# Summed weight pairs in a SwiGLU encoder block: sums on GpSimd, three of eight pairs, a new SBUF layout

## The chip, the cores and the metric

One core of a Trainium2 chip. The metric is the device time of one execution, in microseconds. Most executions of this kernel agree within a few tenths of a per cent.

## What is computed

One encoder layer on 256 tokens of width 2048, all in fp32:

```python
x = x + W_out [ MLA(h) || DiffAttn(h) ]      # h = rms_norm(x), one input projection
x = x + CrossAttn(rms_norm(x), rms_norm(mem))
hf = rms_norm(x, g_ffn)
x = x + (silu(hf @ w_gate) * (hf @ w_up)) @ w_down    # 2048 -> 5632 -> 2048
return rms_norm(x, g_final)
```

The change works in the last line but one, the feed-forward part, and in where tiles lie.

## The kernel before

**Split operands.** Each fp32 matrix is held as a high part (`h`, rounded to fp32r) and a low part (`l`, what is left). `mm` (L89) makes one product out of three matmuls: high x high (L91), high x low (L92), low x high (L93). `split_into` (L97) makes the parts: ScalarE casts the high one (L99), VectorE subtracts it from the source (L100).

**Weights.** Every weight is loaded once from HBM in pieces of 1 MB, by the SP queue, into one of three raw tiles `wraw` (128 x 2048). Two calls of `split_into` turn a raw tile into two pairs of tiles `wh` and `wl` (128 x 1024, four of each, used in turn). TensorE streams these as the moving operand; the activations, transposed and split, are the stationary one.

**The feed-forward part.** The hidden width 5632 is one narrow chunk of 512 columns and five wide chunks of 1024. A wide chunk (`wide_chunk`) is a gate pass and an up pass over eight K pairs (a pair is 256 rows of K), each pass a `wide_project`: four accumulators in PSUM, one raw tile per pair. Then silu(gate) x up is transposed into four new K pairs for the down projection. Down passes (`wide_add`) follow in three groups, after chunks 0, 1-2 and 3-4; the last 1024 output columns of the last group go through the simpler `project`.

**Plain and summed pairs.** A plain pair (kind P) is a 2 x 2 grid of blocks times a 2 x 2 grid: 8 products. A summed pair (kind W) is made in Winograd's way with 7 products from sums of blocks: `summed_pair` makes the sums of the activations once, and `wide_project` makes four sums of the weight blocks for each raw tile, on VectorE: one instruction of 1024 columns (L707) and two of 512 (L711, L712) into `tsum`. The sums have to be split too: 3.5 tiles of 1024 columns a summed pair, 2 a plain one. Of the four sums' split tiles one pair lies in a buffer of its own (`wsum`). Four of the seven products go into PSUM tiles of their own (`q`), which VectorE combines in `leave` once the last summed pair is done; `join` (L744 in gate and up passes) adds an accumulator to the result.

The kinds are `GU_KINDS = "PPWPWPPP"` for gate and up (2 of 8 summed) and `DN_KINDS = "PP" + "PPPW" * 5` for down.

**Silu.** In a wide chunk ScalarE takes the sigmoid of the gate result (L824) and VectorE multiplies it in (L825).

**GpSimd** does the angle tables at the start, small powers, and near the end the multiplication with the final gain (L870); it also issues the transfer of that gain (L865).

**Order.** Engines run their own queues in order. The order within each queue is set when the program is built, by a planner with its own cost estimates that may move instructions of independent tiles past each other. Weight loads keep the program's order (`keep_in_program_order`).

**SBUF.** Pools are laid one behind the other: `const`, then the weights `wp`, then `act` and the smaller ones; `tp`, `soft` and `wsum` are opened in turn.

Of the kernel before, what the change touches and what calls it, by code (L numbers as in the profile page):

```python
# [11 lines left out]
F32 = mybir.dt.float32  # L12
# [7 lines left out]
P = 128  # L20
# [54 lines left out]
def encoder_block(ctx: ExitStack, tc: tile.TileContext, a, out):  # L75
    nc = tc.nc
    PS = bass.MemoryType.PSUM
    const = ctx.enter_context(tc.tile_pool(name="const", bufs=1))
    wp = ctx.enter_context(tc.tile_pool(name="wp", bufs=3))
    act = ctx.enter_context(tc.tile_pool(name="act", bufs=24))  # L80
    sb = ctx.enter_context(tc.tile_pool(name="sb", bufs=2))
    small = ctx.enter_context(tc.tile_pool(name="small", bufs=4))
# [3 lines left out]
    tp = tables.enter_context(tc.tile_pool(name="tp", bufs=1))  # L86

# [19 lines left out]
    def act_tile(shape=(P, 4, S), name="act"):  # L107
# [3 lines left out]
        )  # L111

    def weights(src, fine=False, pool=None, before_k=None, cut=None, raw=None):

        nk, ncols = src.shape[1:]
        begun = raw is not None
        if not begun:  # L120
            raw = wp.tile([P, 2048], F32, name="wraw", tag="wraw", bufs=3)
        raw = raw[:, :nk * ncols].rearrange("p (k c) -> p k c", k=nk)
        step = 1 if fine else nk
        for k in range(0, nk, step):
            if before_k is not None:
                before_k(k)
            if begun and k == 0:
                continue
            tc.keep_in_program_order(nc.sync.dma_start(out=raw[:, k:k + step, :], in_=src[:, k:k + step, :]))
        ks = []  # L130
        step = max(1, 1024 // ncols // 2 * 2)
        for k in range(0, nk, step):
            n = min(step, nk - k)
            if pool:
                w = pool((P, n, ncols), "w")
            else:
                w = [wp.tile([P, 1024], F32R, name=x, tag=x, bufs=4)[:, :n * ncols].rearrange("p (k c) -> p k c", k=n)
                     for x in ("wh", "wl")]
                w = Split(*w)
# [26 lines left out]
    def nat(name):  # L166
        return sb.tile([P, 512], F32, name=name, tag="nat", bufs=7)

# [17 lines left out]
    LAT = KVL + DR  # L186
    lat_raw = wp.tile([P, 2048], F32, name="wraw", tag="wraw", bufs=3)
    for c0, c1 in ((0, QL), (QL, QL + LAT)):
# [12 lines left out]
    NF = DR // 2 + DD // 2  # L201
    posi = const.tile([P, NT], I32, name="posi")
    invf = const.tile([P, NF], F32, name="invf")
    ident = const.tile([P, P], F32, name="ident")
# [60 lines left out]

    posf = const.tile([P, NT], F32, name="posf")
    nc.gpsimd.tensor_copy(out=posf, in_=posi)
# [79 lines left out]

    cosr = const.tile([P, NT, 2, DR // 2], F32, name="cosr")
    sinr = const.tile([P, NT, 2, DR // 2], F32, name="sinr")
    cosd = const.tile([P, NT, 2, DD // 2], F32, name="cosd")  # L350
    sind = const.tile([P, NT, 2, DD // 2], F32, name="sind")

# [31 lines left out]
    soft_pool = ExitStack()  # L384
    soft = soft_pool.enter_context(tc.tile_pool(name="soft", bufs=2))

# [100 lines left out]
    for hg in range(2):  # L487
        t = act_tile(name="mixT")
        mixT.append(t)
        for hp in range(2):  # L490
            ps = [scores([qT[hg][:, h, :], qrT[:, 2 * hg + hp, :]], [kT[hg][:, h, :], krT[:, h % 2, :]])
                  for h in (2 * hp, 2 * hp + 1)]
# [13 lines left out]
                                   op0=ALU.add, op1=ALU.subtract)  # L506
    gdb = const.tile([P, DV], F32, name="gdb")
    tc.keep_in_program_order(nc.sync.dma_start(out=gdb, in_=a["g_diff_sub"].partition_broadcast(P)))
# [124 lines left out]
    soft_pool.close()  # L633
    wsum = ctx.enter_context(tc.tile_pool(name="wsum", bufs=1))


    def pair_raw(src):
        raw = wp.tile([P, 2048], F32, name="wraw", tag="wraw", bufs=3)
        raw = raw.rearrange("p (b c) -> p b c", b=4)
        tc.keep_in_program_order(nc.sync.dma_start(out=raw, in_=src))  # L640
        return raw

    def w_tile(n=2, pool=None):

        pool, tags, bufs = (wp, ("wh", "wl"), 4) if pool is None else (pool, ("wh2", "wl2"), 1)
        return Split(*[pool.tile([P, 1024], F32R, name=x, tag=x, bufs=bufs)[:, :n * 512].rearrange(
            "p (b c) -> p b c", b=n) for x in tags])

    def split_blocks(src, pool=None):
        w = w_tile(src.shape[1], pool)  # L650
        split_into(w, src)
        return w

# [26 lines left out]
    def wide_project(pairs, src, order, leave, join):  # L680

        accs = [[pacc.tile([P, 512], F32, name="acc", tag="acc") for _ in range(2)] for _ in range(NT)]
        used = [[False] * 2 for _ in range(NT)]
        summed = [i for i in order if pairs[i].forms is not None]  # L690
        Q = {}
        for n, i in enumerate(order):
            stop = n == len(order) - 1
            raw = pair_raw(src[i])
            if i not in summed:
                w = [split_blocks(raw[:, 2 * k:2 * k + 2, :]) for k in range(2)]
                for tt in range(NT):
                    for oc in range(2):
                        for k in range(2):
                            mm(accs[tt][oc], pairs[i].at(k, tt), w[k][:, oc, :], not used[tt][oc], stop and k == 1)  # L700
# [6 lines left out]
            nc.vector.tensor_tensor(out=t[:, 0:2, :], in0=raw[:, 1:3, :],  # L707
                                    in1=raw[:, 0:1, :].to_broadcast([P, 2, 512]), op=ALU.add)
            t13 = split_blocks(t[:, 0:2, :])
            b21 = split_blocks(raw[:, 3:4, :])  # L710
            nc.vector.tensor_tensor(out=t[:, 2, :], in0=t[:, 0, :], in1=raw[:, 2, :], op=ALU.add)  # L711
            nc.vector.tensor_tensor(out=t[:, 3, :], in0=t[:, 2, :], in1=raw[:, 3, :], op=ALU.add)  # L712
# [3 lines left out]
            mm(Q[1], A11, b11[:, 0, :], *own)  # L716
            mm(accs[0][1], S3, b11[:, 1, :], False, stop)
            mm(Q[5], S5, t13[:, 0, :], *own)
            mm(Q[7], S7, t13[:, 1, :], *own)
            mm(accs[0][0], A12, b21[:, 0, :], False, stop)  # L720
            mm(Q[6], S6, t24[:, 0, :], *own)
            mm(accs[1][0], A22, t24[:, 1, :], False, stop)
# [51 lines left out]
    def normalized_pairs():  # L774
# [12 lines left out]
        for i, kind in enumerate(GU_KINDS):  # L787
            xr = x2raw[i // 2][:, i % 2 * 2:i % 2 * 2 + 2, :]
            if kind == "P":
                if n == 4:  # L790
                    t, n = act_tile(name="x2n"), 0
                split_into(t[:, n:n + 2, :], xr)
                pairs.append(Pair(t[:, n:n + 2, :]))
                n += 2
            else:
                pairs.append(summed_pair(xr[:, :, :P], xr[:, :, P:]))
        return pairs

    def narrow_chunk(c):
# [5 lines left out]
        for tt in range(NT):  # L805
            r = rstdf[:, tt:tt + 1]
            sg = nat("sg")
            nc.scalar.activation(sg, ga[tt], AF.Sigmoid, scale=r)
            nc.vector.scalar_tensor_tensor(out=sg, in0=ga[tt], scalar=r, in1=sg, op0=ALU.mult, op1=ALU.mult)
            h = nat("h")  # L810
# [6 lines left out]
    def wide_chunk(c, spare):  # L817

        g = wide_result(xn, a["w_gu"][c, 0], GU_SEQ)
        for tt in range(NT):  # L820
            for oc in range(2):
                sg = nat("sg")
                gs = g[tt][:, oc, :]
                nc.scalar.activation(sg, gs, AF.Sigmoid)  # L824
                nc.vector.tensor_tensor(out=gs, in0=gs, in1=sg, op=ALU.mult)  # L825
        u = wide_result(xn, a["w_gu"][c, 1], GU_SEQ)
# [179 lines left out]
```

## Time and profile before

| what | value |
|---|---|
| median of 3 runs | 1158.55 us (1158.5 to 1159.19) |
| profiled execution | 1158.9 us, of which the span is 1157.1 us |
| TensorE / VectorE / ScalarE / GpSimd busy | 1148.1 / 901.3 / 611.0 / 69.3 us |
| granted TensorE clock | 0.999 |
| HBM read | 219.11 MB, 191 GB/s with the writes over the span |

Busy time is the time in which an engine had an instruction in it. TensorE's matmuls overlap each other, so the step from one start to the next says how fast it goes, not the duration of one. The feed-forward part runs from about 460 us to the end.

### The profile page before, as it was taken

The numbers are of one execution on the slowest core, as the hardware profiler recorded it, in microseconds if no ns is written. First come the engines' busy times: TensorE is split into PE (matmuls) and PEld (weight loads), VectorE is DVE, ScalarE is ACT, GpSimd is POOL, SyncE is SP. The second block draws the span as 40 slices with busy tenths as digits, with TensorE's granted clock in tenths as the row PEclk, the third lists the DMA queues.
The fourth block names the chain that finished last, engine by engine and source line by source line (L and its number), as shares of the span: only waits on it lengthen the run. The fifth ranks groups of instructions, "written<-read, shape, count | busy, mean of one in ns | idle before, by whom it ended". The sixth has DMA issues, their size and how long they took to land.

```text
span 1157.1 us, 14401 instructions
## 1 busy us (share of the span) xinstructions
PE 1148.1 (99%) x5510; PEld 961.7 (83%) x5510; DVE 901.3 (78%) x1197; ACT 611.0 (53%) x863; POOL 69.3 (6%) x81
## 2 busy tenths in 40 slices
PE   9999999999999999999999999999999999999997
PEld 7888888888888888888888888888888888888887
DVE  7698766586867776978888787797888788798873
ACT  6755454554665565655444554564544554554552
POOL 4920000001000000000000000000000000000021
PEclk9999999999999999999999999999999999999999
DMA  9565344435755445465565555645556555555651
GB/s 356 215 218 189 113 145 168 161 146 206 272 212 182 146 149 187 174 218 182 185 214 184 206 184 192 218 181 183 202 179 223 204 181 202 192 220 202 210 204 73
DMA packets 33764, 222.13 MB, mean 192 GB/s; under 512 B 4128, under 2 KB 4896, under 8 KB 8992
## 3 DMA queue, kind: packets, MB, share of 16 engines
q1 hardware_dynamic: 32256, 216.86, 52.4%
q0 software_dynamic: 864, 3.15, 0.7%
q10 hardware_dynamic: 576, 1.21, 0.3%
q8 instruction: 43, 0.70, 0.2%
q14 instruction: 25, 0.20, 0.1%
HBM read 219.11 MB, written 2.10 MB: 191 GB/s over the span
## 4 chain that ended last, share of the span: by engine, by line
PE 98%; DMA 1%; issue 0%; DVE 0%; SPq 0%; ACT 0%; POOLq 0%; POOL 0%; DVEq 0%; ACTq 0%
PE acc L92 28%; PE acc L91 28%; PE acc L93 28%; PE q L91 2%; PE q L92 2%; PE q L93 2%; PE pt L315 2%; PE ppt L462 1%; DMA wraw<-in_w_in_lat 1%; PE psc L93 1%; PE psc L91 1%; PE psc L92 1%; PE pt L838 0%; PE acckv L93 0%; PE acckv L92 0%
## 5 line engine op out<-in xcount | busy, mean ns | idle before, releaser
L99 ACT CAST wh<-wraw 128x1024 fp32r<-128x1024 f32 (+2 forms) x399 | 399.2, 1013 | 383.1 <-PE acc L93 346.7
L100 DVE TENSOR_TENSOR wl<-wraw,wh 128x1024 fp32r<-128x1024 f32 (+2 forms) x399 | 469.0, 1184 | 166.3 <-ACT wh L99 164.4
L92 PE MATMUL acc<-wl,x2n_h 128*128 128x512 f32 x480 | 185.5, 390 | 0.0
L93 PE MATMUL acc<-wh,x2n_l 128*128 128x512 f32 x480 | 185.2, 389 | 0.0
L91 PE MATMUL acc<-wh,x2n_h 128*128 128x512 f32 x480 | 160.3, 390 | 0.0
L93 PEld LDWEIGHTS acc<-wh,x2n_l 128*128 128x128 f32 x480 | 90.1, 188 | 18.8
L91 PEld LDWEIGHTS acc<-wh,x2n_h 128*128 128x128 f32 x480 | 90.1, 188 | 18.8
L92 PEld LDWEIGHTS acc<-wl,x2n_h 128*128 128x128 f32 x480 | 90.1, 188 | 18.7
L92 PE MATMUL acc<-wl,hT_h 128*128 128x512 f32 (+1 forms) x272 | 103.7, 381 | 0.0
L93 PE MATMUL acc<-wh,hT_l 128*128 128x512 f32 (+1 forms) x272 | 103.5, 381 | 0.0
L91 PE MATMUL acc<-wh,hT_h 128*128 128x512 f32 (+1 forms) x272 | 89.4, 382 | 0.0
L92 PE MATMUL acc<-wl,x0T_h 128*128 128x512 f32 x224 | 88.2, 395 | 0.0
L93 PE MATMUL acc<-wh,x0T_l 128*128 128x512 f32 x224 | 87.8, 393 | 0.0
L91 PE MATMUL acc<-wh,x0T_h 128*128 128x512 f32 x224 | 87.4, 396 | 0.3 <-ACT x0T_h L102 0.3
L99 ACT CAST wh<-tsum 128x1024 fp32r<-128x1024 f32 x56 | 58.3, 1047 | 42.2 <-DVE tsum L712 30.8
L100 DVE TENSOR_TENSOR wl<-tsum,wh 128x1024 fp32r<-128x1024 f32 x56 | 67.9, 1218 | 9.2 <-ACT wh L99 9.1
L91 PEld LDWEIGHTS acc<-wh,hT_h 128*128 128x128 f32 x272 | 51.2, 188 | 9.9 <-issue 0.2
L93 PEld LDWEIGHTS acc<-wh,hT_l 128*128 128x128 f32 x272 | 51.2, 188 | 9.6
L92 PEld LDWEIGHTS acc<-wl,hT_h 128*128 128x128 f32 x272 | 51.2, 188 | 9.4
L91 PEld LDWEIGHTS acc<-wh,x0T_h 128*128 128x128 f32 x224 | 42.2, 189 | 9.2 <-ACT x0T_h L102 1.2
L92 PEld LDWEIGHTS acc<-wl,x0T_h 128*128 128x128 f32 x224 | 42.3, 189 | 7.9 <-DVE wl L100 0.4
L93 PEld LDWEIGHTS acc<-wh,x0T_l 128*128 128x128 f32 x224 | 42.2, 188 | 7.6
(363 smaller groups left out, 2005.9 us busy)
## 6 DMA issues: line engine op xcount, KB each, us to landing
wraw<-in_w_gu SPq DMA_DIRECT2D x80, 1024.0 KB, 4.8
wraw<-in_w_dn SPq DMA_DIRECT2D x36, 1024.0 KB, 4.8
wraw<-in_w_in SPq DMA_DIRECT2D x24, 1024.0 KB, 4.8
wraw<-in_w_out SPq DMA_DIRECT2D x16, 1024.0 KB, 4.8
wraw<-in_w_down SPq DMA_DIRECT2D x8, 1024.0 KB, 4.8
wraw<-in_w_in_lat SPq DMA_DIRECT2D x7, 832.0 KB, 7.8
wraw<-in_w_xk SPq DMA_DIRECT2D x4, 1024.0 KB, 6.1
wraw<-in_w_xq SPq DMA_DIRECT2D x4, 1024.0 KB, 4.8
```

Of the source, the lines that this page charges most:

```text
L91: nc.tensor.matmul(o, l.h, r.h, start=start, stop=False)
L92: nc.tensor.matmul(o, l.h, r.l, start=False, stop=False)
L93: nc.tensor.matmul(o, l.l, r.h, start=False, stop=stop)
L99: last_cast[0] = nc.scalar.copy(out=dst.h, in_=src).ins
L100: last_split[0] = nc.vector.tensor_tensor(out=dst.l, in0=src, in1=dst.h.bitcast(F32), op=ALU.subtract).ins
L315: nc.tensor.transpose(out=pt[:, j * P:(j + 1) * P], in_=src[:, j * P:(j + 1) * P], identity=ident)
L462: nc.tensor.transpose(out=pt[:, kt * S + tt * P:kt * S + (tt + 1) * P], in_=p[:, tt, kt * P:(kt + 1) * P], identity=ident)
```

## The change

Five things change together.

1. The four weight sums of a summed pair are made by GpSimd, as four instructions of 512 columns, one of them in place in the raw tile. The order of blocks in the raw tile (`SUMS`) and of the products changes with it.
2. `GU_KINDS` has a third summed pair, in gate and up: 3 of 8.
3. In the feed-forward part there are 4 raw tiles and 5 tiles each of `wh` and `wl`, where there were 3 and 4, and the separate buffer for the last sums is gone. A class `Ring` hands the tiles out in turn and takes in the additional ones when attention's memory is free. There are two `tsum` tiles of 1024 columns and one of 512.
4. Pools are put at two ends of SBUF: split weights first at the low end (`side="left"`), with what attention needs above them, in the pool `early`; the rest at the other end. After attention `early` is closed and `late` takes its place. Scratch tiles `nat` are 7 in `early` and 3 in `late`.
5. ScalarE's own silu takes the place of sigmoid and VectorE's multiplication.

```diff
-GU_KINDS = "PPWPWPPP"
+GU_KINDS = "PPWPWPWP"
...
-PLAIN, SUMS = ((0, 0), (0, 1), (1, 0), (1, 1)), ((0, 1), (0, 0), (1, 1), (1, 0))
+PLAIN, SUMS = ((0, 0), (0, 1), (1, 0), (1, 1)), ((0, 0), (1, 1), (1, 0), (0, 1))
...
-    const = ctx.enter_context(tc.tile_pool(name="const", bufs=1))
-    wp = ctx.enter_context(tc.tile_pool(name="wp", bufs=3))
-    act = ctx.enter_context(tc.tile_pool(name="act", bufs=24))
...
+    wp = ctx.enter_context(tc.tile_pool(name="wp", bufs=1, side="left"))
+    const = ctx.enter_context(tc.tile_pool(name="const", bufs=1, side="right"))
+    wr = ctx.enter_context(tc.tile_pool(name="wr", bufs=1, side="right"))
...
+    act = ctx.enter_context(tc.tile_pool(name="act", bufs=24, side="right"))
...
+    attention = ExitStack()
+    early = attention.enter_context(tc.tile_pool(name="early", bufs=1, side="left"))
...
+    class Ring:
+        def __init__(self, name, cols, dtype):
+            self.name, self.cols, self.dtype, self.slots, self.made = name, cols, dtype, [], 0
+        def more(self, pool, n):
+            self.slots = [(pool, f"{self.name}{self.made + i}") for i in range(n)] + self.slots
+            self.made += n
+        def next(self, name=None):
+            self.slots.append(self.slots.pop(0))
+            pool, tag = self.slots[-1]
+            return pool.tile([P, self.cols], self.dtype, name=name or self.name, tag=tag, bufs=1)
...
+    w_raw.more(wr, 3)
+    w_high.more(wp, 4)
+    w_low.more(wp, 4)
+    nat_pool = [early, 7]
...
     soft_pool.close()
-    wsum = ctx.enter_context(tc.tile_pool(name="wsum", bufs=1))
...
+    attention.close()
+    late = ctx.enter_context(tc.tile_pool(name="late", bufs=1, side="left"))
+    nat_pool[:] = late, 3
+    w_high.more(late, 1)
+    w_low.more(late, 1)
+    w_raw.more(late, 1)
...
-            t = wsum.tile([P, 4, 512], F32, name="tsum", tag="tsum", bufs=1)
-            b11 = split_blocks(raw[:, 1:3, :])
-            nc.vector.tensor_tensor(out=t[:, 0:2, :], in0=raw[:, 1:3, :],
-                                    in1=raw[:, 0:1, :].to_broadcast([P, 2, 512]), op=ALU.add)
-            t13 = split_blocks(t[:, 0:2, :])
-            b21 = split_blocks(raw[:, 3:4, :])
-            nc.vector.tensor_tensor(out=t[:, 2, :], in0=t[:, 0, :], in1=raw[:, 2, :], op=ALU.add)
-            nc.vector.tensor_tensor(out=t[:, 3, :], in0=t[:, 2, :], in1=raw[:, 3, :], op=ALU.add)
-            t24 = split_blocks(t[:, 2:4, :], wsum)
+            t = late.tile([P, 2, 512], F32, name="tsum", tag="tsum", bufs=2)
+            T4 = late.tile([P, 1, 512], F32, name="tsum4", tag="tsum4", bufs=1)
+            B11, B22, B21, B12 = [raw[:, b, :] for b in range(4)]
+            T3, T2 = [t[:, b, :] for b in range(2)]
+            for o, x, y in ((T3, B12, B22), (B12, B12, B11), (T2, B12, B22), (T4[:, 0, :], T2, B21)):
+                nc.gpsimd.tensor_tensor(out=o, in0=x, in1=y, op=ALU.add)
+            b11, b22, b21, t1 = split_blocks(raw)
+            t3, t2, t4 = split_blocks(t) + split_blocks(T4)
...
-            nc.scalar.activation(sg, ga[tt], AF.Sigmoid, scale=r)
-            nc.vector.scalar_tensor_tensor(out=sg, in0=ga[tt], scalar=r, in1=sg, op0=ALU.mult, op1=ALU.mult)
+            nc.scalar.activation(sg, ga[tt], AF.Silu, scale=r)
...
-                sg = nat("sg")
-                gs = g[tt][:, oc, :]
-                nc.scalar.activation(sg, gs, AF.Sigmoid)
-                nc.vector.tensor_tensor(out=gs, in0=gs, in1=sg, op=ALU.mult)
+                nc.scalar.activation(g[tt][:, oc, :], g[tt][:, oc, :], AF.Silu)
```

More of the change, by code (lines that the diff above doesn't have):

```diff
@@ L120, in weights @@
         if not begun:
-            raw = wp.tile([P, 2048], F32, name="wraw", tag="wraw", bufs=3)
+            raw = w_raw.next()
         raw = raw[:, :nk * ncols].rearrange("p (k c) -> p k c", k=nk)
@@ L133, in weights @@
             n = min(step, nk - k)
[L134 to L139, printed above, removed]
+            w = pool((P, n, ncols), "w") if pool else split_tile(n, ncols)
             if fine:
@@ L166, in nat @@
     def nat(name):
-        return sb.tile([P, 512], F32, name=name, tag="nat", bufs=7)
+        pool, bufs = nat_pool
+        return pool.tile([P, 512], F32, name=name, tag="nat", bufs=bufs)
     def ps_tile(name):
@@ L186, in encoder_block @@
     LAT = KVL + DR
-    lat_raw = wp.tile([P, 2048], F32, name="wraw", tag="wraw", bufs=3)
+    lat_raw = w_raw.next()
     for c0, c1 in ((0, QL), (QL, QL + LAT)):
@@ L201, in encoder_block @@
     NF = DR // 2 + DD // 2
-    posi = const.tile([P, NT], I32, name="posi")
-    invf = const.tile([P, NF], F32, name="invf")
+    posi = early.tile([P, NT], I32, name="posi")
+    invf = early.tile([P, NF], F32, name="invf")
     ident = const.tile([P, P], F32, name="ident")
@@ L261, in encoder_block @@
                 mm(acc_kv[tt][:, :LAT], x, w[:, QL:], i + k == 0, i == 7 and k == 1)
-    posf = const.tile([P, NT], F32, name="posf")
+    posf = early.tile([P, NT], F32, name="posf")
     nc.gpsimd.tensor_copy(out=posf, in_=posi)
@@ L384, in encoder_block @@
     soft_pool = ExitStack()
-    soft = soft_pool.enter_context(tc.tile_pool(name="soft", bufs=2))
+    soft = soft_pool.enter_context(tc.tile_pool(name="soft", bufs=2, side="left"))
     def diff_rope(acc):
@@ L506, in encoder_block @@
                                    op0=ALU.add, op1=ALU.subtract)
-    gdb = const.tile([P, DV], F32, name="gdb")
+    gdb = early.tile([P, DV], F32, name="gdb")
     tc.keep_in_program_order(nc.sync.dma_start(out=gdb, in_=a["g_diff_sub"].partition_broadcast(P)))
@@ L633, in encoder_block, with split_blocks @@
     soft_pool.close()
-    wsum = ctx.enter_context(tc.tile_pool(name="wsum", bufs=1))
[L637 to L652, printed above, removed]
+    attention.close()
[4 more added lines that the diff above has]
+    w_raw.more(late, 1)
+    def split_blocks(x):
+        blocks = []
+        for i in range(0, x.shape[1], 2):
+            n = min(2, x.shape[1] - i)
+            w = split_tile(n, 512)
+            split_into(w, x[:, i:i + n, :])
+            blocks += [w[:, j, :] for j in range(n)]
+        return blocks
     class Pair:
@@ L693, in wide_project @@
             stop = n == len(order) - 1
-            raw = pair_raw(src[i])
+            raw = w_raw.next().rearrange("p (b c) -> p b c", b=4)
+            tc.keep_in_program_order(nc.sync.dma_start(out=raw, in_=src[i]))
             if i not in summed:
-                w = [split_blocks(raw[:, 2 * k:2 * k + 2, :]) for k in range(2)]
+                w = split_blocks(raw)
                 for tt in range(NT):
@@ L699, in wide_project @@
                         for k in range(2):
-                            mm(accs[tt][oc], pairs[i].at(k, tt), w[k][:, oc, :], not used[tt][oc], stop and k == 1)
+                            mm(accs[tt][oc], pairs[i].at(k, tt), w[2 * k + oc], not used[tt][oc], stop and k == 1)
                             used[tt][oc] = True
@@ L789, in normalized_pairs @@
             if kind == "P":
-                if n == 4:
+                if n == 4 and "P" in GU_KINDS[i + 1:]:
                     t, n = act_tile(name="x2n"), 0
+                elif n == 4:
+                    t = Split(*[late.tile([P, 2, S], F32R, name="odd" + x, tag="odd" + x, bufs=1) for x in "hl"])
+                    n = 0
                 split_into(t[:, n:n + 2, :], xr)
```

31 lines of the change are left out of this document (17 added, 14 removed).

## The prediction

> **What bounds the kernel now.** I read the page first, then the busy time by windows, then the waits, then the chain.
>
> ```profile
> span 1157.1 us, 14401 instructions
> PE 1148.1 (99%) x5510; PEld 961.7 (83%) x5510; DVE 901.3 (78%) x1197; ACT 611.0 (53%) x863; POOL 69.3 (6%) x81
> PE   9999999999999999999999999999999999999997
> PE 98%; DMA 1%; issue 0%; DVE 0%; SPq 0%; ACT 0%; POOLq 0%; POOL 0%; DVEq 0%; ACTq 0%
> ```
>
> TensorE is busy in every slice and is 98% of the chain that ended last. A busy TensorE need not be one at its peak, so I look at windows of the feed-forward part. 641 to 726 and 899 to 984 us each hold one 1024-column chunk: a gate pass, an up pass, the transposes.
>
> ```profile
> 560.00:1143.00 583.00, 583.00 (x2668) 484.22 (x2667) 475.16 (x557) 293.06 (x345) 12.89 (x8) 1.00 0.54 192
> 641.00:726.00 85.00, 85.00 (x377) 70.04 (x376) 68.36 (x78) 42.70 (x48) 0.00 (x0) 1.00 0.55 196
> 899.00:984.00 85.00, 85.00 (x378) 70.07 (x377) 68.58 (x77) 42.70 (x48) 0.00 (x0) 1.00 0.56 197
> ACT wh L99 <- PE acc L93: 358.0, 220, 7.1
> SPq L640 <- DVE wl L100: 575.2, 115, 9.7
> ```
>
> The columns are the window, then busy time of PE, PEld, DVE, ACT and POOL, granted clock, DMA share, GB/s. PE is never idle in 583 us at clock 1.00. The cover around it: in a chunk of 85.0 us DVE works 68.4 (80%), ACT 42.7 (50%), GpSimd nothing. The first wait says that ScalarE's casts wait for matmuls to free a split tile, the second that the weight loads wait for VectorE's splits to free a raw tile: supply is paced by TensorE. A matmul taken out therefore shortens the run, as long as the supply keeps up.
>
> **The matmuls.**
>
> ```profile
> 499.69 0.91 PE acc L91 x4
> 535.16 0.70 PE q L91 x3
> L91 PE MATMUL acc<-w_h,hT_h 128*128 128x256 f32 x24 | 6.8, 283 | 0.0
> L91 PE MATMUL acc<-wh,hT_h 128*128 128x256 f32 x24 | 6.8, 283 | 0.0
> ```
>
> The first two are pieces of the chain: a step is 0.91/4 = 0.2275 us among plain matmuls, 0.70/3 = 0.233 at the dearest among the products of a summed pair. A plain pair is 8 products of 3 matmuls (24), a summed pair 7 products (21). One pair of eight turns from plain to summed in each of 5 chunks x 2 passes: 30 matmuls, 30 x 0.2275 = 6.8 us less. On the other side, if all 21 matmuls of the ten new summed pairs run at the dearer step, that is 10 x 21 x 0.0055 = 1.2 us more; I take it whole. If, instead, five split tiles smooth these steps everywhere, the 28 old summed pairs give back up to 28 x 21 x 0.0055 = 3.2.
>
> The new place of the split weights: w_h and wh are split weights out of two different pools, thus from different places in SBUF, and the matmul that streams them takes 283 ns from both. Nothing here shows that the place counts; I put 0, with no bound seen on either side other than these equal rows.
>
> **VectorE and ScalarE.**
>
> ```profile
> L100 DVE TENSOR_TENSOR wl<-wraw,wh 128x1024 fp32r<-128x1024 f32 x354 | 432.0, 1228 | 152.4 <-ACT wh L99 150.5
> L99 ACT CAST wh<-wraw 128x1024 fp32r<-128x1024 f32 x354 | 368.4, 1052 | 353.3 <-PE acc L93 322.9 <-issue 10.3 <-PE q L93 4.9
> L707 DVE TENSOR_TENSOR tsum<-wraw 128x1024 f32<-128x1024 f32 x28 | 34.1, 1218 | 2.9 <-DMA wraw<-in_w_dn 2.2 <-DMA wraw<-in_w_gu 0.2
> L711 DVE TENSOR_TENSOR tsum<-tsum,wraw 128x512 f32<-128x512 f32 x28 | 19.1, 683 | 0.1
> L712 DVE TENSOR_TENSOR tsum<-tsum,wraw 128x512 f32<-128x512 f32 x28 | 19.1, 683 | 0.2
> L825 DVE TENSOR_TENSOR res<-res,sg 128x512 f32<-128x512 f32 x20 | 13.1, 681 | 0.0
> L824 ACT ACTIVATE sg<-res 128x512 f32<-128x512 f32 x20 | 12.2, 627 | 9.1 <-DVE res L744 9.0
> ```
>
> Per chunk VectorE loses the sums of 4 summed pairs, 4 x (1.218 + 0.683 + 0.683) = 10.3 us, and four multiplications of the silu, 4 x 0.68 = 2.7. Two plain pairs become summed: a plain one splits 2 tiles of 1024 columns, a summed one 3.5, so 2 x 1.5 x 1.228 = 3.7 us come. 68.4 - 13.0 + 3.7 = 59.1 us of its own, in a chunk that is now 85.0 - 6 x 0.2275 = 83.6 (71%). ScalarE gets 2 x 1.5 x 1.052 = 3.2: 45.9 of 83.6. Neither is on the path: 0.
>
> Silu takes sigmoid's place one for one, so 0.627 us a call stays.
>
> ```profile
> 466.02 1.28 ACT L808 ACT_TABLE_LOAD   x1
> L671 DVE TENSOR_TENSOR sums<-x2T_f x2: 279/280/280, 466.8 to 468.5; 128x128 f32<-128x128 f32 x2
> L100 DVE TENSOR_TENSOR forms_l<-sums,forms_h x7: 675/678/683, 480.3 to 1081.2; 128x512 fp32r<-128x512 f32 x7
> ```
>
> One table load stands ahead of the first sigmoid; in its place one stands ahead of the first silu. At worst the squares at the end need another, 1.28 us on an engine that is half idle: 0. The third summed activation pair costs VectorE four subtractions of 0.28 and about 0.8 of splitting more, once, under the narrow chunk's matmuls: 0, about 2 if that cover is gone.
>
> **GpSimd and what it does to VectorE.** 38 summed tiles (28 + 10) x 4 sums. GpSimd's only such instruction in the trace is the one near the end, at L870:
>
> ```profile
> L870 POOL TENSOR_TENSOR xres<-xres,gfb x6: 1293/2071/2369, 1103.9 to 1132.3; 128x512 f32<-128x512 f32 x6
> 1103.86 1.29 POOL L870 TENSOR_TENSOR xres<-xres,gfb 128x512 f32<-128x512 f32 x1 [73.24 <-ACT junk L183]
> 1106.19 6.43 POOL L870 TENSOR_TENSOR xres<-xres,gfb 128x512 f32<-128x512 f32 x3 [1.04 <-ACT junk L183]
> 1105.69 1.22 DVE L100 TENSOR_TENSOR wl<-wraw,wh 128x1024 fp32r<-128x1024 f32 x1
> 1107.09 2.05 DVE L100 TENSOR_TENSOR wl<-wraw,wh 128x1024 fp32r<-128x1024 f32 x1 [0.18 <-ACT wh L99]
> 1110.25 3.46 DVE L100 TENSOR_TENSOR wl<-wraw,wh 128x1024 fp32r<-128x1024 f32 x2 [1.10 <-ACT wh L99]
> 1131.43 2.01 DVE L100 TENSOR_TENSOR w_l<-wraw,w_h 128x1024 fp32r<-128x1024 f32 x1 [0.23 <-ACT w_h L99]
> ```
>
> Alone it takes 1.29 us. Beside VectorE's splits three of them take 6.43, and a split that normally takes 1.22 takes 2.05, 2.01, and one of the pair about 2.1: the two engines take turns. Six GpSimd instructions lengthened three splits, by 0.83, 0.9 and 0.79: 0.42 us of VectorE lost for each GpSimd instruction on average, 0 at best, 1.29 (all of it) at worst. That is the unknown of this change. A chunk has 6 summed tiles, 24 GpSimd sums. VectorE's need becomes 59.1 + 24 x loss: 69.2 us (83%) at 0.42, 73.5 (88%) at 0.6, 90.1 (108%) at 1.29. It equals the chunk's 83.6 at a loss of (83.6 - 59.1)/24 = 1.02. I take 0.6, above the average seen because VectorE is busier inside a chunk than at the end. Then TensorE still bounds it, and the sums cost 0. The down passes have two summed tiles of eight as before, so less of this.
>
> The Trainium skill, "SBUF — State Buffer", section "Who interferes with whom", says that a VectorE instruction with two SBUF inputs contends with a GpSimd one that reads SBUF, and that whoever comes first holds the port for the whole instruction. By the 2.05 against 1.22 the trace agrees. The splits have two SBUF inputs, so by this rule alone every sum could cost VectorE its whole length, which is the first rival.
>
> The chain of four sums must also be ready in time:
>
> ```profile
> wraw<-in_w_gu SPq DMA_DIRECT2D x80, 1024.0 KB, 4.8
> POOL gfb L865 <- PE acc L93: 590.2, 1, 590.2
> ```
>
> A raw tile lands 4.8 us after its issue; four sums need 5.2 us alone, 4 x 6.43/3 = 8.6 in turns: 13.4 us from issue to the last sum. Four raw tiles last TensorE about 4 x 83.6/16 = 20.9 us, so some 7 us are over for the last splits. No wait of TensorE follows: 0. What queues behind a late sum is ScalarE's cast of it, with later tiles' casts behind that. The sums are also queued on GpSimd with the transfer of the final gain, which waits for a matmul to free its buffer; sums of the last passes may stand behind it. A sum stays ready about 7 us early, so I put 0, up to 5 us once.
>
> Three small scratch tiles in place of seven in the feed-forward part hold sums, residual parts and h, all of them short-lived: 0.
>
> **The sum**, against the profiled execution (1158.9 us, span 1157.1): 1158.9 - 6.8 + 1.2 = 1153.3. The median of the runs is 0.35 lower than that execution: 1153.0.
>
> **Rivals.**
>
> - VectorE becomes the bound through the shared port (slower). It decides from a loss of 1.02 us per sum upward. For it: sums come four in a row, splits two in a row, and in such a spell the engines alternate strictly (6.43 us for three); each chunk's summed tiles now stand at places 3, 5 and 7, so spells crowd. Against it: VectorE also has instructions that read PSUM, and gaps, under which a sum is free; half of the six cost nothing. At a loss of 1.15 a chunk needs 86.7 us, 3.1 over TensorE's 83.6, times 5: 1153.0 + 15.5 = 1168. The end, 1.29, gives 90.1, +32: 1185.
> - The sums come late for the queues that run in a fixed order. ScalarE stands at a cast of a sum and TensorE runs dry at summed tiles. A quarter of a microsecond at each of 38 is 9.5: 1162. Against it are the 7 us of lead.
> - The change does nothing to the end: waits at the ten pass ends, where VectorE must join four accumulators before TensorE reuses them, eat the gain, 0.5 us each: 1158.
>
> **How the numbers follow.** Forecast 0.64, shared port 0.20, late sums 0.11, gain eaten 0.05. What a measurement of this kernel tells from no change is about 0.2%, 2.3 us; the forecast lies 5.5 below the median. Faster 0.64, same 0.05, slower 0.31. The range: down to 1149, with the dear steps gone (1153.0 - 1.2 - 3.2 = 1148.6), up to 1170, past the first rival's own time; what its worse half and the second rival's tail have above is left out. The forecast's own range is 1149 to 1156.
>
> **What would show it.** Right: PE still busy in all of the feed-forward windows, a chunk of 83.6 to 83.9 us; 30 fewer matmuls; VectorE's busy time per chunk 69 to 76 us with splits of 2.0 among those of 1.22; GpSimd's sums at 1.3 to 2.3 us; no wait of PE for VectorE among the longest. Wrong: waits of PE for wl at L100 or for the joins at L744, a chunk of 86 us or more with VectorE over 95%, casts of sums waiting for GpSimd, or a matmul step other than 0.227 us.

## The result and the profile after

The changed kernel takes 1208.54 us (median of 6 runs, 1202.2 to 1210.6), the kernel before 1158.75 (6 runs): ratio 1.0417, 95% interval 1.0391 to 1.0444. It is 4.2% slower where 0.5% faster was forecast, and outside the range. The profiled execution took 1210.6 us, of which the span is 1208.6.

The page of the changed kernel:

```profile
span 1208.6 us, 14533 instructions
PE 1159.0 (96%) x5480; PEld 962.7 (80%) x5480; DVE 938.9 (78%) x1117; ACT 627.5 (52%) x885; POOL 350.6 (29%) x233
PE   9999999999999999999998999999999999999997
PEclk9999999999999999999998999999999999999999
PE 79%; DVE 13%; issue 4%; ACT 2%; DMA 1%; SPq 0%; POOLq 0%; POOL 0%; DVEq 0%; ACTq 0%
```

The 30 matmuls are gone (5510 to 5480). But TensorE has only 79% of the chain, VectorE 13%. The span grew by 51.5 us. TensorE's idle time went from 1157.1 - 1148.1 = 9.0 to 1208.6 - 1159.0 = 49.6: 40.6 us of it. Its busy time grew by 10.9 although 6.8 us of matmuls are missing, so the others took 17.7 longer. The mean granted clock fell from 0.999 to 0.986; 0.013 of 1208.6 us is 15.7.

The waits say for whom TensorE stood (in total, times, longest). Below them are two windows with the same columns as before: one over a chunk with the end of a down pass and its stall ahead of it, and one over the chunk alone.

```profile
PE acc L95 <- DVE res L770: 18.4, 10, 2.8
PE acc L96 <- DVE wl L104: 7.0, 6, 1.8
PE acc L95 <- DVE xres L794: 6.9, 2, 4.0
PEld acc L95 <- ACT sg L837: 4.6, 1, 4.6
640.00:736.00 96.00, 89.52 (x384) 73.31 (x383) 78.92 (x64) 46.58 (x51) 47.67 (x27) 0.96 0.49 176
648.20:738.10 89.90, 85.81 (x366) 70.23 (x367) 72.82 (x60) 45.63 (x50) 41.63 (x23) 0.97 0.51 185
```

L770 and L794 are the joins, in gate and up passes and in down passes: TensorE wants an accumulator for the next pass before VectorE has read it. That is 25.3 us of some 40, at the ends of all ten gate and up passes of the wide chunks and of two down passes. Another 7.0 us are waits for splits (L104), and one stall is for silu (L837). Yet VectorE works only 78.9 of 96.0 us (82%) in the longer window and 72.8 of 89.9 (81%) in the chunk alone. It is not the bound on average; it is late at certain places.

One such place, the end of a down pass, in the timelines of VectorE, GpSimd and TensorE (start, duration, instruction, idle time before it):

```profile
917.77 2.31 DVE L104 TENSOR_TENSOR wl<-wraw,wh 128x1024 fp32r<-128x1024 f32 x1
920.01 1.78 DVE L790 TENSOR_TENSOR xres<-xres,v 128x512 f32<-128x512 f32 x1
921.71 1.77 DVE L791 TENSOR_TENSOR xres<-xres,v 128x512 f32<-128x512 f32 x1
923.40 1.21 DVE L104 TENSOR_TENSOR wl<-wraw,wh 128x1024 fp32r<-128x1024 f32 x1
924.54 2.47 DVE L794 TENSOR_TENSOR xres<-xres,acc 128x512 f32<-128x512 f32 x4
917.38 1.62 POOL L737 TENSOR_TENSOR wraw<-wraw 128x512 f32<-128x512 f32 x1
919.07 2.16 POOL L737 TENSOR_TENSOR tsum<-wraw 128x512 f32<-128x512 f32 x1
921.31 1.62 POOL L737 TENSOR_TENSOR tsum<-tsum,wraw 128x512 f32<-128x512 f32 x1
925.36 0.47 PE L95 MATMUL acc<-wh,x2n_h 128*128 128x512 f32 x1 [2.85 <-DVE xres L794]
```

While GpSimd makes the sums for the next pass, one split takes 2.31 us instead of 1.22 and two additions to the residual 1.78 and 1.77 instead of 0.68. That is 1.09 + 1.10 + 1.09 = 3.3 us, by which the joins behind them in VectorE's queue are held back. TensorE waits 2.85 us.

What follows such a stall, in the chain and in windows:

```profile
926.62 0.43 PE acc L96
930.16 0.23 PE acc L96
922.00:925.50 3.50, 0.65 (x4) 0.26 (x3) 3.50 (x4) 1.86 (x2) 1.46 (x2) 1.00 0.61 257
925.50:932.00 6.50, 6.50 (x22) 5.19 (x23) 5.40 (x5) 0.00 (x0) 4.17 (x3) 0.74 0.33 108
```

A matmul takes 0.43 us instead of 0.23 for some 3.4 us after the stall; the granted clock in that window is 0.74. The profile has eight such spells, most of 3.4 us, but not behind every stall: 2.44 us at 692 us has none behind it (clock 1.00 from 694.8 to 710 us), while waits of 1.14 and 1.31 us close together at 787 us have. It differs between executions too: those of 1202.2 and 1203.9 us had a granted clock of 0.992, the other four 0.986 or 0.987. The Trainium skill, "TensorE: Matmul & The Clock Gate", Part 1, describes this: TensorE's clock falls to half after an idle window of about 3.4 us and comes back after as long a busy one. The doubled step agrees; the idle time ahead of it here was 2.85 us, less than the page's window.

The terms of VectorE and GpSimd by groups:

```profile
L104 DVE TENSOR_TENSOR wl<-wraw,wh 128x1024 fp32r<-128x1024 f32 x382 | 532.4, 1412 | 178.4 <-ACT wh L103 176.6
L104 DVE TENSOR_TENSOR wl<-tsum,wh 128x1024 fp32r<-128x1024 f32 x38 | 56.0, 1474 | 0.8 <-ACT wh L103 0.8
L104 DVE TENSOR_TENSOR wl<-tsum,wh 128x512 fp32r<-128x512 f32 x38 | 35.1, 923 | 7.8 <-ACT wh L103 7.8
L857 DVE TENSOR_TENSOR res<-res,res 128x512 f32<-128x512 f32 x20 | 17.6, 917 | 0.0
L737 POOL TENSOR_TENSOR tsum<-wraw 128x512 f32<-128x512 f32 x76 | 139.3, 1833 | 281.6 <-DMA wraw<-in_w_gu 174.3 <-DMA wraw<-in_w_dn 104.3
L737 POOL TENSOR_TENSOR tsum<-tsum,wraw 128x512 f32<-128x512 f32 x38 | 73.1, 1923 | 118.7 <-DVE wl L104 117.5
L737 POOL TENSOR_TENSOR wraw<-wraw 128x512 f32<-128x512 f32 x38 | 72.8, 1915 | 3.0
```

Against 1.228, 1.218, 0.685 and 0.681 us before, these four groups of VectorE's instructions with two SBUF inputs lost 382 x 0.184 + 38 x 0.256 + 38 x 0.238 + 20 x 0.236 = 93.8 us beside 152 sums: 0.62 us a sum.

### The profile page after: what moved, and what is told of

The parts are those of the page before. It is cut to its first block, busy times and chain, and to the rows that moved or that the text cites. A ratio compares the mean times of both kernels' runs of the same rounds, so it can differ in the third digit from the quotient of the medians.

```text
span 1208.6 us, 14533 instructions
## 1 busy us (share of the span) xinstructions
PE 1159.0 (96%) x5480; PEld 962.7 (80%) x5480; DVE 938.9 (78%) x1117; ACT 627.5 (52%) x885; POOL 350.6 (29%) x233
## 4 chain that ended last, share of the span: by engine, by line
PE 79%; DVE 13%; issue 4%; ACT 2%; DMA 1%; SPq 0%; POOLq 0%; POOL 0%; DVEq 0%; ACTq 0%
PE acc L96 22%; PE acc L95 22%; PE acc L97 22%; DVE wl L104 8%; PE q L95 2%; PE q L96 2%; PE q L97 2%; ACT wh L103 2%; PE pt L342 1%; DVE res L770 1%; DVE res L857 1%; PE ppt L489 1%; PE psc L97 1%; PE psc L96 1%; PE psc L95 1%
## 5 line engine op out<-in xcount | busy, mean ns | idle before, releaser
L104 DVE TENSOR_TENSOR wl<-wraw,wh 128x1024 fp32r<-128x1024 f32 (+2 forms) x399 | 550.0, 1397 | 188.1 <-ACT wh L103 186.3
L103 ACT CAST wh<-wraw 128x1024 fp32r<-128x1024 f32 (+2 forms) x399 | 410.3, 1041 | 351.4 <-PE acc L97 254.9
L737 POOL TENSOR_TENSOR tsum<-wraw 128x512 f32<-128x512 f32 x76 | 139.3, 1833 | 281.6 <-DMA wraw<-in_w_gu 174.3
L95 PE MATMUL acc<-wh,x2n_h 128*128 128x512 f32 x320 | 120.7, 412 | 24.6 <-DVE res L770 13.5
L96 PE MATMUL acc<-wl,x2n_h 128*128 128x512 f32 x320 | 129.6, 405 | 0.0
L97 PE MATMUL acc<-wh,x2n_l 128*128 128x512 f32 x320 | 128.8, 403 | 0.0
L737 POOL TENSOR_TENSOR tsum<-tsum,wraw 128x512 f32<-128x512 f32 x38 | 73.1, 1923 | 118.7 <-DVE wl L104 117.5
L95 PEld LDWEIGHTS acc<-wh,x2n_h 128*128 128x128 f32 x320 | 63.7, 199 | 42.5 <-issue 16.5
L104 DVE TENSOR_TENSOR wl<-tsum,wh 128x1024 fp32r<-128x1024 f32 x76 | 89.7, 1198 | 8.6 <-ACT wh L103 8.6
L103 ACT CAST wh<-tsum 128x1024 fp32r<-128x1024 f32 x76 | 63.2, 835 | 53.9 <-issue 29.6
L97 PEld LDWEIGHTS acc<-wh,x2n_l 128*128 128x128 f32 x320 | 62.9, 197 | 13.7
L737 POOL TENSOR_TENSOR wraw<-wraw 128x512 f32<-128x512 f32 x38 | 72.8, 1915 | 3.0
L96 PEld LDWEIGHTS acc<-wl,x2n_h 128*128 128x128 f32 x320 | 62.9, 197 | 13.0
```

Source lines behind the costliest of these rows:

```text
L95: nc.tensor.matmul(o, l.h, r.h, start=start, stop=False)
L96: nc.tensor.matmul(o, l.h, r.l, start=False, stop=False)
L97: nc.tensor.matmul(o, l.l, r.h, start=False, stop=stop)
L103: last_cast[0] = nc.scalar.copy(out=dst.h, in_=src).ins
L104: last_split[0] = nc.vector.tensor_tensor(out=dst.l, in0=src, in1=dst.h.bitcast(F32), op=ALU.subtract).ins
L737: nc.gpsimd.tensor_tensor(out=o, in0=x, in1=y, op=ALU.add)
```

## The experiments

The theories: **port** (a GpSimd sum holds back VectorE's instructions with two SBUF inputs; at a pass end the joins are behind them), **lateness** (the sums are ready too late), **crowding** (the third summed pair next to the pass end puts too much on VectorE there, whoever makes the sums). Later came **lead** (a fourth raw tile brings the next pass's work onto the end of the pass before) and **scratch** (three scratch tiles are too few). Each run stands beside the kernel before on the same chip, 1158.7 to 1159.2 us.

### Whose sums, and how many

```diff
# e1_sums_on_vector
-                nc.gpsimd.tensor_tensor(out=o, in0=x, in1=y, op=ALU.add)
+                nc.vector.tensor_tensor(out=o, in0=x, in1=y, op=ALU.add)
```

> The changed kernel with its four weight sums on VectorE, all else as changed (3 of 8, rings of 4 and 5, layout, silu). Port theory (a GpSimd sum holds the SBUF port that VectorE's instructions with two SBUF inputs need, and VectorE's joins at a pass end come late): splits go back to 1.22 us, VectorE's own need in a chunk is 59 + 24 x 0.68 = 75 us of 84, the stalls at the pass ends go, 1150 to 1156 us. Crowding theory (a third summed pair beside the pass end puts too much on VectorE there, whoever makes the sums): the stalls of 2 to 4 us at the pass ends stay, 1180 to 1205.

Measured: 1185.91 us, ratio 1.0247 (1.0219 to 1.0275). The sums cost 22.6 us more on GpSimd than on VectorE; 27 of the 50 us stay with them on VectorE. The crowding theory's range was met, the port theory's was not. But the stalls of 2 to 4 us at the pass ends did not stay as such; TensorE's two longest groups of waits in this run:

```profile
PE acc L95 <- DVE res L770: 6.8, 7, 2.3
PE q L95 <- ACT wh L103: 5.7, 5, 1.1
```

The waits for these joins fell from 18.4 to 6.8 us, and the longest from 2.8 to 2.3; those for casts ahead of a product (L103) rose to 5.7. At the end of an up pass VectorE's queue shows why joins are still late:

```profile
726.65 0.68 DVE L737 TENSOR_TENSOR tsum<-tsum,wraw 128x512 f32<-128x512 f32 x1
727.25 0.69 DVE L770 TENSOR_TENSOR res<-acc,res 128x512 f32<-128x512 f32 x1
727.85 1.22 DVE L104 TENSOR_TENSOR wl<-wraw,wh 128x1024 fp32r<-128x1024 f32 x1
729.58 0.69 DVE L770 TENSOR_TENSOR res<-acc,res 128x512 f32<-128x512 f32 x1
```

Sums and splits for the next pass stand before and between the joins, though nobody needs them yet.

```diff
# e2_two_of_eight
-GU_KINDS = "PPWPWPWP"
+GU_KINDS = "PPWPWPPP"
```

> The changed kernel with 2 of 8 pairs summed in gate and up, as before the change, sums still on GpSimd. Port theory: a chunk has 16 GpSimd sums instead of 24 and none near the pass end, 30 matmuls (6.8 us) come back; a third to two thirds of the 50 us goes: 1170 to 1190. Crowding theory: the stalls at the ends of gate and up passes go, those of the down passes stay, about 1160 to 1168.

Measured: 1170.54, ratio 1.0091 (1.0072 to 1.0110), at the lower end of the port theory's range. The third pair is worth 38 us. What stays are three stalls of 2.85 us, all at the ends of down passes, as the crowding theory had it. In the profiled execution, 1166.42 us, the clock stayed at 1.00 behind all three, so a stall of this length does not always bring the slow clock.

```diff
# e3_gpsimd_sums_alone, in the kernel before: L707, L711 and L712
-            nc.vector.tensor_tensor(out=t[:, ...
+            nc.gpsimd.tensor_tensor(out=t[:, ...
```

> The kernel before with its three sum instructions (1024, 512, 512 columns) on GpSimd and nothing else changed. Port theory: with 28 summed tiles, 112 sums of 512 columns in all, the splits beside them grow to 2 us and more, 1165 to 1190. Lateness theory (the chain on GpSimd is too slow for the split tiles behind it): one tsum tile and 3 raw tiles leave no lead, TensorE waits at the summed tiles themselves, over 1190. Crowding theory: no more than 1162, since the pass ends are as before.

Measured: 1160.75, ratio 1.0013 (1.0004 to 1.0023). Sums on GpSimd cost next to nothing in the old surroundings: below the port theory's range, as the crowding theory had it, and TensorE does not wait for late sums, with one `tsum` tile and three raw tiles.

### Is it the port, or the lateness

GpSimd works for nobody, VectorE makes the real sums:

```diff
# e4_shadow_sums, on e1
+            idle = sb.tile([P, 512], BF16, name="junk", tag="junk", bufs=1)
+            for x, y in ((B11, B22), (B22, B21), (B21, B11), (B11, B22)):
+                nc.gpsimd.tensor_tensor(out=idle, in0=x, in1=y, op=ALU.add)
```

> The changed kernel with its sums on VectorE, while GpSimd adds blocks of the same raw tiles, four instructions of 512 columns for each summed pair, into a bf16 scratch tile that nobody reads (more work is done, none left out). Nobody waits for a GpSimd result here, save that the raw tile is freed after its reads. Port theory: as slow as the changed kernel or slower, 1200 to 1240, with waits of TensorE for VectorE at the pass ends. Lateness theory: as fast as with the sums on VectorE alone, 1150 to 1160.

Measured: 1292.34, ratio 1.1147 (1.1129 to 1.1165). 106 us over e1 for sums that nobody waits for: for these 106 us lateness is out. A raw tile is held longer, though, so:

```diff
# e6_shadow_apart, on e1
+            nc.gpsimd.tensor_copy(out=idle[:, :1], in_=raw[:, 0, :1])
+            wide = ident.unsqueeze(1).to_broadcast([P, 4, P])
+            for _ in range(4):
+                nc.gpsimd.tensor_tensor(out=idle..., in0=wide, in1=wide, op=ALU.add)
```

> As the run with the shadow sums, 3 of 8 with the real sums on VectorE, but GpSimd's four idle additions of 512 columns for each summed pair read a constant tile instead of the raw tile, after one copy of a single column of the raw tile that starts them. The raw tile no longer waits for GpSimd. Port theory: nearly all of the loss of the shadow sums stays, 1250 to 1300. If the loss came from raw tiles held longer: 1183 to 1200, like the sums on VectorE alone.

Measured: 1262.89, ratio 1.0886 (1.0858 to 1.0914). The groups of this run:

```profile
L740 POOL TENSOR_TENSOR junk<-ident 128x512 bf16<-128x512 f32 x152 | 230.7, 1518 | 12.0
L742 DVE TENSOR_TENSOR tsum<-wraw 128x512 f32<-128x512 f32 x76 | 76.6, 1011 | 23.6 <-DMA wraw<-in_w_gu 12.3 <-DMA wraw<-in_w_dn 11.0
```

But for the copy of one column, GpSimd's instructions share no data with VectorE's, and VectorE's sums `tsum<-wraw` still go from 0.69 us (e1) to 1.01. 77 of the 106 us stay, 0.51 us for each idle addition. The granted clock fell from 0.996 in e1 to 0.970, which is 4.7 us lost there and 37.9 here: some 33 of the 77 us are slow clock behind the stalls. The port theory is shown. The other 29 us fit raw tiles held longer, but an idle addition also took 1.91 us in e4 and 1.52 here; the two were not tried apart.

### The place of the summed pairs

```diff
# e7_early_on_vector, on e1; e8_early_on_gpsimd, on the changed kernel
-GU_KINDS = "PPWPWPWP"
+GU_KINDS = "PWPWPWPP"
```

> 3 of 8 with the sums on VectorE, and the summed pairs at places 2, 4 and 6 of the pass (PWPWPWPP) instead of 3, 5 and 7. Pass-end theory: with two plain pairs behind the last summed one, as before the change, the joins come in time, stalls at the ends of gate and up passes go, and the 30 matmuls count: 1151 to 1162. If VectorE's need as such is too large (75 us of 84 in a chunk): 1175 to 1190, as with PPWPWPWP.

Measured: 1171.56, ratio 1.0104 (1.0089 to 1.0119), against 1185.91 with PPWPWPWP.

> The changed kernel, sums on GpSimd, with the summed pairs at places 2, 4 and 6 (PWPWPWPP). Pass-end theory: part of the stalls goes, 1160 to 1185, the rest being GpSimd's hold on the port for the next pass's first summed pair, whose sums now fall on the pass end even more. Need-as-such theory: about 1205, no change.

Measured: 1175.74, ratio 1.0131 (1.0105 to 1.0156), against 1208.54. The place alone is worth 14 us on VectorE and 33 on GpSimd, with the same instructions. e7 missed its range, since the remaining stalls were not those of the pass ends that I had in mind: 4.8 us for silu at 481 us, the rest mostly for splits and casts.

### The other parts

```diff
# e5_two_on_vector: e1 with GU_KINDS = "PPWPWPPP"
# e11_silu_alone: the kernel before with silu, here and in the narrow chunk
...
-                nc.scalar.activation(sg, gs, AF.Sigmoid)
-                nc.vector.tensor_tensor(out=gs, in0=gs, in1=sg, op=ALU.mult)
+                nc.scalar.activation(g[tt][:, oc, :], g[tt][:, oc, :], AF.Silu)
```

> The changed kernel with 2 of 8 pairs summed and the sums on VectorE: what is left of the change is rings, layout, silu and the order of products. Pass-end theory (TensorE waits where VectorE's joins at a pass end come late, from the third summed pair beside the pass end and from GpSimd holding the port, in addition): no stall left, 1156 to 1160 us. If the rings or the layout cost something of their own: 1163 or more.

Measured: 1161.60, ratio 1.0021 (1.0011 to 1.0030). Rings, layout, silu and order together cost 2.4 us, a little above the 1156 to 1160 expected.

> The kernel before with ScalarE's own silu and nothing else changed. All theories: silu takes sigmoid's time and VectorE's 20 multiplications go, where VectorE has room: 1158 to 1160, no change. If the silu table cost reloads between calls: 10 or more extra table loads of 1.28 us in ScalarE's queue, still little in time.

Measured: 1159.09, ratio 1.0003 (0.9994 to 1.0013): nothing, as all expected.

### Scratch and lead

In the runs so far with three summed pairs TensorE stands 4 to 5 us at 481 us for silu. ScalarE's queue there, in the changed kernel:

```profile
482.39 1.13 ACT L103 CAST forms_h<-sums 128x512 fp32r<-128x512 f32 x2
483.54 1.28 ACT L837 ACT_TABLE_LOAD   x1
484.83 0.69 ACT L837 ACTIVATE sg<-acc,x2Tr 128x512 f32<-128x512 f32 x1
```

Silu stands behind the casts of summed activations and its own table load. First attempt:

```diff
# e9_early_silu_first on e8, e10_early_vector_silu_first on e7, behind ga
+        sgs = act.tile([P, NT, 512], F32, name="sgs", tag="act")
+        for tt in range(NT):
+            nc.scalar.activation(sgs[:, tt, :], ga[tt], AF.Silu, scale=rstdf[:, tt:tt + 1])
         xn = normalized_pairs()
...
-            sg = nat("sg")
-            nc.scalar.activation(sg, ga[tt], AF.Silu, scale=r)
+            sg = sgs[:, tt, :]
```

> As the run with summed pairs at places 2, 4 and 6 and the sums on GpSimd, but the narrow chunk's silu is issued right behind its gate product, into tiles of the large activation pool instead of one of the three scratch tiles. Scratch theory (the 5 us stall at 483 us comes from silu waiting for a scratch tile that a summed activation pair still holds): that stall and the slow clock behind it go, 6 to 8 us less than 1175.7, 1165 to 1170. If ScalarE is late there for its own work: no change.

> The same edit on the run with the sums on VectorE (summed pairs at places 2, 4 and 6). Scratch theory: 6 to 8 us less than 1171.6: 1162 to 1166. The rest over 1152 is then TensorE waiting for splits behind VectorE's sums, many small waits.

Measured: 1173.07 (ratio 1.0124, 1.0109 to 1.0139) and 1171.85 (1.0116, 1.0101 to 1.0131). Both missed: the wait moved. In e9 TensorE now stood 3.2 us at 477 us for a split and 1.5 us for the transposes of `h`, which takes a scratch tile too; in e10 it stood 3.8 us for these transposes.

```diff
# e12_gate_order, on e9
-        g = wide_result(xn, a["w_gu"][c, 0], GU_SEQ)
+        g = wide_result(xn, a["w_gu"][c, 0], (0, 2, 1, 3, 4, 5, 6, 7))
```

> As the run with silu first and sums on GpSimd, and the gate passes take the pairs in the order P P W W P W P P (the up passes stay P W P W P W P P). Port theory: after a down pass GpSimd's first sums come one tile later and collide less with VectorE's combining and joining there; the stalls of about 3 us at those places shrink: 3 to 8 us less than without this order, 1157 to 1164. Two summed pairs in a row may cost some of it, as they need eight of five split tiles.

Measured: 1173.04, ratio 1.0126 (1.0109 to 1.0143). A miss: the stall at 477 us went, but two behind the down passes grew from 2.4 to 3.9 us. One tile later, GpSimd's sums lay on the residual additions right ahead of the joins (1.78 and 1.77 us), so it was not late enough.

Then the memory itself:

```diff
# e14_two_three_raw, on e2; e17 on the changed kernel, e18 on e7
-    w_raw.more(late, 1)
# e13_three_raw on the changed kernel, e15 on e8, e16 on e7: this as well
-    nat_pool[:] = late, 3
+    nat_pool[:] = late, 7
```

> The run with 2 of 8 pairs on GpSimd, with 3 raw tiles instead of 4 and nothing else. Lead theory: its three stalls of 3.2 us at the ends of down passes go, 1160 to 1163 instead of 1170.5. Otherwise: 1170 or more.

Measured: 1157.48, ratio 0.9984 (0.9975 to 0.9993). 13 us less than e2, and under the expected range. The end of the same down pass, first e2, then e14:

```profile
892.39 1.78 DVE L790 TENSOR_TENSOR xres<-xres,v 128x512 f32<-128x512 f32 x1
896.92 2.47 DVE L794 TENSOR_TENSOR xres<-xres,acc 128x512 f32<-128x512 f32 x4
888.27 1.41 POOL L737 TENSOR_TENSOR tsum<-wraw 128x512 f32<-128x512 f32 x1 [19.58 <-DMA wraw<-in_w_gu]
```

```profile
883.83 0.68 DVE L789 TENSOR_TENSOR xres<-xres,v 128x512 f32<-128x512 f32 x1
886.17 2.50 DVE L793 TENSOR_TENSOR xres<-xres,acc 128x512 f32<-128x512 f32 x4
884.52 2.89 POOL L736 TENSOR_TENSOR tsum<-wraw 128x512 f32<-128x512 f32 x1 [16.27 <-DMA wraw<-in_w_gu]
```

With 4 raw tiles GpSimd begins 896.92 - 888.27 = 8.7 us before the joins, and the residual additions take 1.78 us. With 3 it begins 1.7 us before them, and they take 0.68. The joins read an accumulator in PSUM beside one SBUF input and are not slowed by GpSimd's sums beside them in either. The lead theory is shown here.

> The changed kernel with 3 raw tiles as before the change instead of 4, and seven scratch tiles in the feed-forward part in the room that this frees. Scratch theory: the 4.6 us stall at 481 us goes. Lead theory (the fourth raw tile brings GpSimd's sums onto the pass end before): the stalls of 3 to 4.4 us at the ends of down passes go too, those beside the third summed pair of gate and up passes stay; 1182 to 1195 in all. If neither holds: 1205 or more, as three raw tiles give less lead to the sums.

Measured: 1177.80, ratio 1.0161 (1.0145 to 1.0176): a little better than expected. What TensorE waits for has changed, though, and the chain shows one of the two longest stalls:

```profile
PE acc L95 <- DVE res L769: 2.1, 1, 2.1
PE q L95 <- ACT wh L103: 7.1, 2, 3.6
760.02 4.76 DMA wraw<-in_w_gu
764.87 1.06 ACT wh L103
765.97 0.50 PE q L95
```

The joins (L769) make TensorE wait only once. The two longest stalls, both at ends of gate passes, end with the cast of a raw tile whose transfer could start only at 760.02 us here, 2.5 us before the stall. With three raw tiles and the third pair at place 7 lead is short there.

> The changed kernel with 3 raw tiles instead of 4 and nothing else (scratch tiles stay 3). Lead theory: most of the 31 us came from the raw tile, 1180 to 1187, with the 4.6 us stall at 481 us still there. Scratch theory for the bulk: 1195 or more.

Measured: 1185.16, ratio 1.0222 (1.0207 to 1.0238). So taking the fourth raw tile away gives back 23.4 us of the changed kernel, and four more scratch tiles 7.4. The place of the latter, 476 to 486 us, in e17 and then in e13, by windows:

```profile
476.00:486.00 10.00, 5.78 (x25) 4.42 (x24) 9.71 (x11) 6.04 (x8) 5.34 (x3) 0.97 0.85 315
476.00:486.00 10.00, 10.00 (x47) 8.23 (x46) 10.00 (x13) 4.24 (x6) 5.54 (x3) 1.00 0.81 315
```

TensorE's busy time is 5.78 of 10 us with three scratch tiles, 10.00 with seven.

> Summed pairs at places 2, 4 and 6, sums on GpSimd, 3 raw tiles and seven scratch tiles. Both theories: the 5.5 us stall at 482 us and the 3 us stalls at the ends of down passes go, 1157 to 1166 instead of 1175.7. With three raw tiles the sums may come late for a summed pair at place 2, then 1170 or more.

Measured: 1165.63, ratio 1.0057 (1.0042 to 1.0072). Within the first range. Of the stall at 482 us 2.0 us for a cast and 1.1 for silu are left, and the sums come a little late now: TensorE waits 2.0 and 2.1 us for splits at the first gate passes behind down passes.

> Summed pairs at places 2, 4 and 6, sums on VectorE, 3 raw tiles and 3 scratch tiles. Lead theory: the many waits of under 1.3 us go with the raw tile, the 5.2 us stall at 481 us stays with the scratch tiles: 1159 to 1164, between 1154.8 (3 raw, 7 scratch) and 1171.6 (4 raw, 3 scratch). Scratch theory for the bulk: 1168 to 1172.

Measured: 1160.69, ratio 1.0013 (1.0003 to 1.0022), as the lead theory had it.

> The same with the sums on VectorE. Scratch theory: the 5.2 us stall at 481 us goes and the slow clock behind it, 1163 to 1166 instead of 1171.6; the many waits of under 1.3 us for splits at summed pairs stay.

Measured: 1154.82, ratio 0.9962 (0.9948 to 0.9976). **This version is faster than both kernels**, by 0.4% than the one before: three of eight pairs summed at places 2, 4 and 6, sums on VectorE, 3 raw tiles, seven scratch tiles, silu and the layout as changed. Its page and two windows, each 84 us inside a chunk:

```profile
span 1153.4 us, 14404 instructions
PE 1142.9 (99%) x5480; PEld 955.3 (83%) x5480; DVE 930.1 (81%) x1269; ACT 627.1 (54%) x885; POOL 68.9 (6%) x81
640.00:724.00 84.00, 83.84 (x377) 69.08 (x377) 74.56 (x89) 46.42 (x53) 0.00 (x0) 1.00 0.56 203
899.00:983.00 84.00, 84.00 (x380) 69.70 (x379) 74.75 (x91) 45.85 (x54) 0.00 (x0) 1.00 0.55 200
```

VectorE is 89% busy there, more than in the changed kernel (81%), and TensorE hardly waits. The expected 1163 to 1166 was too high: I had given the raw tile no part where GpSimd makes no sums, but it was worth 10.9 us there too (1171.56 to 1160.69).

## Why the prediction was wrong

- **The matmuls**: right. 30 fewer, and outside the spells of slow clock the step is still 0.23 us. In e16, where little else stands in the way, TensorE is busy for 5.2 us less (1148.1 to 1142.9), close to the 6.8 less 1.2 of the sum. The span is only 3.7 us shorter, since TensorE's idle time grew from 9.0 to 10.5 us.
- **The layout**: 0 was right as far as it shows. The step did not change, and rings, layout, silu and order together cost 2.4 us (e5). The five split tiles were not varied by themselves.
- **Silu**: right by itself (e11). In the changed kernel its table load, put at 0, lies inside the stall at 481 us with its 1.28 us.
- **The loss for each sum**: 0.6 us was taken, 0.62 measured. VectorE's need in a chunk came out as reckoned, 72.8 us against 73.5. The number I called the unknown of this change was right; that it lay so close was partly luck, as it was chosen between 0 and 1.29 from six instructions.
- **"Then TensorE still bounds it, and the sums cost 0"**: this is the step that failed. I compared VectorE's need with TensorE's over a whole chunk and took anything under 100% for hidden. But TensorE waits for VectorE at a few places, above all the joins at a pass end, and a delay in front of these counts (3.3 us of delay, 2.85 of waiting), however idle VectorE is elsewhere. Instead of 0 the trace has 25.3 us of waits for joins and 7.0 for splits, and slow clock behind them. e16, with 89% and no stall, and the changed kernel, with 81% and 1.3 to 4.0 us at twelve pass ends, show it from both sides.
- **The first rival** had the shared port, but as a bound on average from a loss of 1.02 us a sum; 0.62 was enough to hold up the joins.
- **The third rival** named the place but priced it at 0.5 us a pass end, with nothing to work that out from; the twelve waits were 2.1 us on average and 4.0 at most. I should have listed what stands in VectorE's queue ahead of a join, and which of it has two SBUF inputs.
- **Where the third summed pair stands** had no term. Moved one place forward, with its neighbours, it gives back 14 us (sums on VectorE) or 33 (on GpSimd).
- **The rings**: I counted the fourth raw tile as lead that makes late sums unlikely. In the old surroundings lead was not short (e3 does with three raw tiles); with the third pair at place 7 three were short at two pass ends (e13), but the fourth cost more: it let the next pass's sums and splits go ahead of the joins, 13 us with two summed pairs, 23 with three, 11 with three on VectorE at the earlier places. That the planner puts them there because the tile lands sooner is argued; that the tile costs it is shown (e14, e17, e18).
- **The scratch tiles**: put at 0, "all of them short-lived"; 7.4 us measured. In ScalarE's queue silu stood behind the casts of these sums; that it was held there by the scratch tiles follows from e13 and e17, where their number alone differs.
- **The clock** had no term: eight times a stall, or two close together, was followed by half speed, mostly for 3.4 us. Some 15.7 us went that way. What decides whether a stall brings it stays open.

The parts do not add up independently: against the same sums on VectorE, GpSimd's cost 1.6 us in the old surroundings, 9 with the rings, 22.6 with the third pair as well.

## What to carry to other kernels

An engine's average load doesn't tell whether work moved beside it is hidden. Find the few instructions of that engine for which the bound engine waits, list what stands ahead of them in the queue, and price the change there. More buffers are not a gain by themselves: with queues in order, earlier data lets unneeded work go ahead of needed work.

## What the runs showed of the hardware

GpSimd's additions of 512 columns slowed VectorE even when they read a constant that VectorE did not use (e6: 0.69 to 1.01 us on average for its sums `tsum<-wraw`), while VectorE's joins, which read PSUM, kept their time beside them (2.47 us for four in e2, 2.50 in e14). TensorE's clock fell to half eight times in the changed kernel's profile, after stalls from 1.1 and 1.3 us close together to 4.2 us; behind three of 2.85 us in e2's profile it did not. And 152 such additions whose result is thrown away made the run 77 us longer, some 33 of them by the slow clock, more than the changed kernel lost in all.
